# A two-layer encoder kernel: the first feed-forward matmul as seven block products, and a new order of the second

## The chip, the cores and the metric

The kernel runs on one core of one Trainium2 chip, as one program. The metric is device time in microseconds. A core has TensorE (PE, the matmul engine; PEld is its weight load), VectorE (DVE), ScalarE (ACT), GpSimd (POOL) and SyncE (SP), which here only issues transfers. Each works through its own queue in order.

## The reference, cut to what matters

Two sequences of 512 tokens and 1024 features go through two layers. Each layer ends with a squared-ReLU feed-forward part:

```
for l in range(DEPTH):                                  # DEPTH = 2
    h = x @ w_in[l]                                     # 1024 -> 5376
    ...                                                 # window attention, HGRN2, gates
    x = layer_norm(ALPHA * x + mixed @ w_out[l], ln1_g[l], ln1_b[l])
    ff = jnp.square(jax.nn.relu(x @ w_ff1[l])) @ w_ff2[l]   # 1024 -> 4096 -> 1024
    x = layer_norm(ALPHA * x + ff, ln2_g[l], ln2_b[l])
```

All of it is float32. HGRN2 is a gated linear recurrence over the tokens in both directions, done in blocks of 1 to 64 tokens.

## The kernel before, in words

**Numbers.** A float32 value is kept as a rounded part (hi, type fp32r) and a remainder (lo). One product of two such values is three matmuls: hi·hi, hi·lo, lo·hi (`mm3`, L149 to L154). `split` (L130 to L132) makes the two parts: ACT copies to hi, and POOL or DVE subtracts to get lo. `load_w` (L137) loads a weight column block of 1024 x 128 into a raw tile and splits it into a w tile. There are three raw and three w tiles.

**Tokens.** The 1024 tokens are eight rows of 128; rows 0 to 3 are group g = 0, rows 4 to 7 group g = 1. `Fm` (L156 to L188) holds an activation with features on the partitions. `put` transposes one row: twice four PE transposes into an "sm" PSUM bank, an ACT copy to hi (L185), a DVE subtraction to lo (L186). PSUM has four "mm" and four "sm" banks. `project` (L190) multiplies a weight block with one group, 24 matmuls of 128 x 128 by 128 x 512.

**A layer.** HGRN (`hgrn`, L230) projects its columns (`prep`), woven with the block recurrences (`units`) of the columns before them; `pairs` (L249) sums products within a head by a matmul with a matrix of ones, as hi and lo, first for `ox` and then for `other`, through one pair of tiles. Attention follows, then the gated output projections, `out_proj` (L868) row by row, and a layer norm for each row. Rows of x1 are transposed as they come (L899, L901).

**First feed-forward matmul (FF1).** `ff1` (L908) loads one of 32 column blocks of w_ff1, projects both groups, takes relu on ACT (L915) and the square on DVE (L916). Two blocks are a pair p, 0 to 15. `combine` (L918) makes of a pair's four 128 x 512 results (two blocks, two groups) the seven left operands of a seven-product scheme, some split already, in two pages of 1 MB, and `spill` (L929) writes them to DRAM (`hsp`).

**Second feed-forward matmul (FF2).** It is a 2 x 2 x 2 block matmul done in seven products. `PHASES` (L47) lists them: the PSUM banks ("m" or "s"; "+" adds to the phase before), the slot in `hsp`, one or two blocks of w_ff2, how these are combined, and into which quarters of the output each is folded and with what sign. A phase has 16 steps; each reads an operand from `hsp`, makes the weight operand on POOL, and splits both (`operands`, L946), two steps ahead of `products` (L969, 12 matmuls). Four 1 MB block tiles of each w_ff2 quarter are loaded by `load_block` (L936); the first two quarters from the last four pairs of FF1 on, in slots of the tiles X ("a_tile", eight of 8 KB a partition). The first phase is H_M1, whose weight operand is a sum of two blocks. `fold` (L981) adds a finished bank into the row accumulators, `close` (L994) does the layer norm and stores the row. In the last phase rows 4 to 7 are closed, and transposed as the next layer's input, while its products run; in the last four steps the products go row by row.

What sets the order: Tile's scheduler orders instructions by the program's order and by when their tiles come free; the order on each engine is then fixed. All transfers here go through SP's queue.

## Time and profile before

| | |
|---|---|
| Median of 3 runs | 3021.17 us (3017.67 to 3022.82) |
| The profiled execution's own time | 3024.58 us |
| Its span, first to last instruction | 3022.8 us |
| Mean granted TensorE clock | 0.991 |
| Matmul instructions | 16720 |
| Bytes moved by DMA | 348.75 MB |

The profile shows one execution. Busy times are sums over an engine's instructions; matmuls overlap in it, so the spacing of their starts is what one costs. "Idle before" is the time an engine sat still before an instruction, with what released it. The granted clock 1.00 is 2.4 GHz, 0.50 is 1.2 GHz.

### The profile page before, as it was taken

The page shows a single profiled execution, that of the slowest core. Times are in us where ns is not written, and L with a number is a line of the kernel's source. Part 1 is how long each engine was busy: PE and PEld are TensorE (multiplying, and loading weights), DVE is VectorE, ACT ScalarE, POOL GpSimd, SP SyncE. Part 2 cuts the span into 40 slices and gives each one's busy share as a digit, 9 for nine tenths or more (in the row PEclk, how much of TensorE's full clock was granted, in tenths as well). Part 3 has the DMA queues.
Part 4 walks back from the last instruction along what each step waited for, and adds up shares of the span by engine and source line. Part 5 has one row for each costly group of instructions (what it writes and reads, how often), then busy time and mean ns, then how long its engine had stood idle before and what let it go on. Part 6 is the DMA issues. An engine that isn't in the chain of part 4 may idle for free.

```text
span 3022.8 us, 42662 instructions
## 1 busy us (share of the span) xinstructions
PE 2949.1 (98%) x16720; PEld 2396.3 (79%) x16720; DVE 1614.0 (53%) x2813; ACT 1160.6 (38%) x1954; POOL 862.0 (29%) x532
## 2 busy tenths in 40 slices
PE   8999999999999998999999999999999999989997
PEld 6777787878888887888777777878888888878885
DVE  5777648126543444445668886570265343444447
ACT  3555647423122222343335555573232222224332
POOL 3222120112222222454542221101131222224544
PEclk9999999999999999999999999999999999999999
DMA  3111222246124356533521112322460334474334
GB/s 128 36 43 36 68 86 71 82 160 215 43 91 160 133 188 250 169 97 111 170 70 36 43 43 71 88 67 100 162 225 5 129 130 160 170 283 136 97 122 139
DMA packets 278377, 348.75 MB, mean 115 GB/s; under 512 B 16033, under 2 KB 184609, under 8 KB 269985
## 3 DMA queue, kind: packets, MB, share of 16 engines
q1 hardware_dynamic: 276880, 342.82, 34.3%
q8 instruction: 131, 2.15, 0.3%
q10 hardware_dynamic: 1296, 3.21, 0.3%
q14 instruction: 70, 0.57, 0.1%
HBM read 238.77 MB, written 100.66 MB: 112 GB/s over the span
## 4 chain that ended last, share of the span: by engine, by line
PE 83%; DVE 11%; DMA 2%; issue 1%; ACT 1%; POOL 1%; SPq 0%; POOLq 0%; ACTq 0%; DVEq 0%
PE mm L152 17%; PE mm L154 17%; PE mm L153 17%; PE mm L975 3%; PE mm L976 3%; PE sm L976 3%; PE sm L977 3%; PE sm L975 3%; PE mm L977 3%; PE mm L878 1%; PE mm L877 1%; PE mm L876 1%; PE sm L706 1%; PE sm L652 1%; PE sm L696 1%
## 5 line engine op out<-in xcount | busy, mean ns | idle before, releaser
L152 PE MATMUL mm<-X,w 128*128 128x512 f32 x2624 | 1034.4, 394 | 3.0 <-ACT w L131 2.6
L153 PE MATMUL mm<-X,w 128*128 128x512 f32 x2624 | 1027.5, 392 | 2.2 <-DVE X L186 2.0
L154 PE MATMUL mm<-X,w 128*128 128x512 f32 x2624 | 1027.8, 392 | 1.0 <-POOL w L132 1.0
L132 POOL TENSOR_TENSOR w<-raw,w 128x1024 fp32r<-128x1024 f32 (+1 forms) x179 | 419.1, 2342 | 1346.8 <-ACT w L131 1231.8
L152 PEld LDWEIGHTS mm<-X,w 128*128 128x128 f32 x2624 | 494.0, 188 | 109.2 <-ACT w L131 3.0
L154 PEld LDWEIGHTS mm<-X,w 128*128 128x128 f32 x2624 | 494.0, 188 | 102.5 <-POOL w L132 1.9
L153 PEld LDWEIGHTS mm<-X,w 128*128 128x128 f32 x2624 | 494.1, 188 | 101.9 <-DVE X L186 2.3
L131 ACT CAST w<-raw 128x1024 fp32r<-128x1024 f32 (+1 forms) x330 | 321.4, 975 | 373.8 <-PE sm L977 106.7
L916 DVE TENSOR_TENSOR X<-t 128x512 f32<-128x512 f32 x128 | 88.4, 691 | 390.4 <-ACT t L915 390.4
L132 DVE TENSOR_TENSOR w<-raw,w 128x1024 fp32r<-128x1024 f32 (+1 forms) x153 | 182.3, 1195 | 176.7 <-ACT w L131 176.6
L915 ACT ACTIVATE t<-mm 128x512 f32<-128x512 f32 x128 | 76.3, 596 | 423.0 <-PE mm L154 423.0
L965 POOL TENSOR_TENSOR raw<-X 128x512 f32<-128x512 f32 x128 | 173.6, 1358 | 227.3 <-DVE w L132 226.8
L975 PE MATMUL mm<-w 128*128 128x512 f32 x480 | 190.4, 398 | 27.0 <-ACT w L131 18.0
L976 PE MATMUL mm<-w 128*128 128x512 f32 x480 | 189.9, 396 | 0.1
L977 PE MATMUL mm<-w 128*128 128x512 f32 x480 | 189.4, 395 | 0.0
L975 PE MATMUL sm<-w 128*128 128x512 f32 x384 | 149.5, 389 | 0.0
L976 PE MATMUL sm<-w 128*128 128x512 f32 x384 | 149.4, 389 | 0.0
L977 PE MATMUL sm<-w 128*128 128x512 f32 x384 | 149.4, 389 | 0.0
L975 PEld LDWEIGHTS mm<-w 128*128 128x128 f32 x480 | 91.6, 191 | 50.2 <-ACT w L131 18.9
L359 ACT COPY bd<-Q 64x512 f32<-64x512 f32 x192 | 120.8, 629 | 14.7 <-DVE Q L429 11.8
L805 DVE TENSOR_TENSOR X<-raw,X 128x512 fp32r<-128x512 f32 x32 | 20.8, 689 | 196.0 <-ACT X L804 195.8
L963 POOL TENSOR_TENSOR w<-X,w 128x512 fp32r<-128x512 f32 x64 | 84.6, 1322 | 99.6 <-ACT w L959 98.0
(196 smaller groups left out, 3898.5 us busy)
## 6 DMA issues: line engine op xcount, KB each, us to landing
hsp<-X SPq DMA_DIRECT2D x64, 1024.0 KB
raw<-hsp SPq DMA_DIRECT2D x192, 256.0 KB
raw<-in_w_in_dram SPq DMA_DIRECT2D x84, 512.0 KB
raw<-in_w_ff_dram SPq DMA_DIRECT2D x64, 512.0 KB
X<-in_w_ff_dram SPq DMA_DIRECT2D x32, 1024.0 KB
gates<-gt SPq DMA_DIRECT2D x64, 256.0 KB
t<-gates SPq DMA_DIRECT2D x64, 256.0 KB
w<-hsp SPq DMA_DIRECT2D x24, 512.0 KB
```

The lines of the kernel that those rows point to most:

```text
L131: (first or nc.scalar.copy)(hi, src)
L132: (eng or nc.gpsimd).tensor_tensor(lo, src, hi.bitcast(F32), op=ALU.subtract)
L152: nc.tensor.matmul(ps, ah, bh, start=(i == 0), stop=False)
L153: nc.tensor.matmul(ps, ah, bl, start=False, stop=False)
L154: nc.tensor.matmul(ps, al, bh, start=False, stop=(i == n - 1))
L359: nc.scalar.copy(dst, src[hs])
L916: nc.vector.tensor_tensor(out[g], t, t, op=ALU.mult)
L963: nc.gpsimd.tensor_tensor(w[:, 1, 512:], src, w[:, 0, 512:].bitcast(F32), op=ALU.subtract)
L965: nc.gpsimd.tensor_tensor(raw[:, 512:], block(b0, k), block(b1, k), op=op)
L975: nc.tensor.matmul(ps[r], hh, wh, start=first, stop=False, **kw)
L976: nc.tensor.matmul(ps[r], hh, wl, start=False, stop=False, **kw)
L977: nc.tensor.matmul(ps[r], hl, wh, start=False, stop=stop, **kw)
```

## The change

- FF1 becomes a 2 x 2 x 2 block product too: features in two halves, the two column blocks of a pair, and the two token groups. Seven products of four 128-feature steps (12 matmuls each) replace eight. The right operands, seven of 512 x 512, are transposed and split once a layer: "11" and "21" (the two halves of group 0), "22" (a half of group 1), and four sums t1 to t4 (`sums`, `put_op`). The left operands are sums of weight blocks, made on POOL in the raw tile c and split.
- For the pairs 0 to 4 (`AHEAD`), the two products that need only group 0 ("11", "21") are done before the others, while group 1 is still being summed and transposed; their results go to DRAM (`first_sp`) and are read back in the pair.
- The row sums for the transposes lie in w tiles (rows 0, 3) and in pages (rows 1, 2). The pages of the pairs alternate between two sets, one of X tiles, one of the accumulators of rows 0 to 3, whose contents go to DRAM (`x1_sp`) and come back in FF2's first phase.
- Squares are done on ACT (relu, then square) or as one DVE operation.
- FF2 begins with H_M2 and H_M5, which use one block each; the banks of the phases are exchanged, so that the last phase is in "sm" banks. The first two blocks and the first two steps' operands are issued inside the last pair (`hook`); other blocks come during the first two phases.
- In HGRN, `pairs` is cut in two: the second ones-matmul runs one weave step later. Its tiles are six instead of four, and the gate tiles come from the same pool.

The diff, cut to its core:

```
 PHASES = (
-    ("m", H_M1, (0, 0), (1, 1), ALU.add, ((0, 0, 1), (1, 1, 1))),
     ("s", H_M2, (0, 0), None, None, ((1, 0, 1), (1, 1, -1))),
     ("m", H_M5, (1, 1), None, None, ((0, 0, -1), (0, 1, 1))),
-    ("s", H_M3, (0, 1), (1, 1), ALU.subtract, ((0, 1, 1),)),
-    ("s+", H_M6, (0, 0), (0, 1), ALU.add, ((1, 1, 1),)),
-    ("m", H_M4, (1, 0), (0, 0), ALU.subtract, ((1, 0, 1),)),
-    ("m+", H_M7, (1, 0), (1, 1), ALU.add, ((0, 0, 1),)),
+    ("s", H_M1, (0, 0), (1, 1), ALU.add, ((0, 0, 1), (1, 1, 1))),
+    ("m", H_M3, (0, 1), (1, 1), ALU.subtract, ((0, 1, 1),)),
+    ("m+", H_M6, (0, 0), (0, 1), ALU.add, ((1, 1, 1),)),
+    ("s", H_M4, (1, 0), (0, 0), ALU.subtract, ((1, 0, 1),)),
+    ("s+", H_M7, (1, 0), (1, 1), ALU.add, ((0, 0, 1),)),
 )
...
-                hi, lo = t2k(F32R), t2k(F32R)
-                for w in (ox, other):
-                    ...
+                first = ones_mm(ox)
+                next(first)
+                ps = next(first)
+                other = t2k()
+                ...
+                second = ones_mm(other)
+                next(second)
+                def crosswise():
+                    ps = next(second)
+                    ...
...
+            def put_op(name, r, nat):
+                ps = sm_ps()
+                for k in range(4):
+                    nc.tensor.transpose(ps[:, k * P:(k + 1) * P], nat[:, k * P:(k + 1) * P], ident)
+                pv = ps.rearrange("p (k t) -> p k t", t=P)
+                hi, lo = (t[:, :, r * P:(r + 1) * P] for t in ops[name])
+                nc.scalar.copy(hi, pv)
+                nc.vector.tensor_tensor(lo, pv, hi.bitcast(F32), op=ALU.subtract)
+            def sums(r, t):
+                t1, t2, t3, t4 = t
+                y0, y1 = acc[r], acc[4 + r]
+                nc.gpsimd.tensor_tensor(t3, y1[:, 512:], y1[:, :512], op=ALU.subtract)
+                nc.vector.tensor_tensor(t1, y1[:, :512], y0[:, :512], op=ALU.subtract)
+                nc.vector.tensor_tensor(t2, y1[:, 512:], t1, op=ALU.subtract)
+                nc.vector.tensor_tensor(t4, y0[:, 512:], t2, op=ALU.subtract)
+                return t
+            def left(src, eng, n=2):
+                w = w_tile()
+                split(w[:, 0, :n * 512], w[:, 1, :n * 512], src, eng)
+                ...
+            def times(ps, w, name, start=True, stop=True):
+                hi, lo = ops[name]
+                for k in range(4):
+                    ...                                   # three matmuls
...
+            for p in range(AHEAD):
+                if p >= 2:
+                    pre.append(left(w_cols(2 * p), nc.gpsimd))
+                banks[p] = mm_ps()
+                times(banks[p], pre[p][0], "11")
+                t = t512()
+                nc.scalar.copy(t, banks[p])
+                nc.sync.dma_start(first_sp[p][:, 0], t)
+                if p:
+                    finish_first(p - 1)
+                if p == 2:
+                    made.append(sums(3, in_w()))
+                if p < 4:
+                    put_second(p, made[p])
...
+            def ff1(p, hook):
+                s, h = ([part(t, i) for i in range(4)] for t in sets[p % 2])
+                a, b, c = w_cols(2 * p), w_cols(2 * p + 1), raw_tile()
+                q = slice(0, 512), slice(512, 1024)
+                if p < AHEAD:
+                    u2 = t512()
+                    nc.sync.dma_start(u2, first_sp[p][:, 0])
+                    nc.sync.dma_start(h[0], first_sp[p][:, 1])
+                else:
+                    l11, l12 = left(a, nc.gpsimd)
+                nc.gpsimd.tensor_tensor(c[:, q[0]], b[:, q[0]], b[:, q[1]], op=add)
+                nc.gpsimd.tensor_tensor(c[:, q[1]], c[:, q[0]], a[:, q[0]], op=sub)
+                s1, s2 = left(c, nc.vector)
+                nc.gpsimd.tensor_tensor(b[:, q[0]], a[:, q[0]], b[:, q[0]], op=sub)
+                nc.gpsimd.tensor_tensor(c[:, q[1]], a[:, q[1]], c[:, q[1]], op=sub)
+                s3, l22 = left(b, nc.gpsimd if p < AHEAD else nc.vector)
+                if p >= AHEAD:
+                    p1 = mm_ps()
+                    times(p1, l11, "11")
+                    u2 = t512()
+                    nc.scalar.copy(u2, p1)
+                p6 = sm_ps()
+                times(p6, s2, "t2")
+                hook(0)
+                tt(u2, u2, p6, op=add)
+                if p >= AHEAD:
+                    times(p1, l12, "21", start=False)
+                    banks[p] = p1
+                    first_done(p, h[0])
+                s4, = left(c[:, q[1]], nc.vector, 1)
+                p5 = mm_ps()
+                times(p5, s1, "t1")
+                hook(1)
+                p7 = sm_ps()
+                times(p7, s3, "t3")
+                hook(2)
+                u3 = t512()
+                tt(u3, u2, p7, op=add)
+                tt(h[3], u3, p5, op=add)
+                square_act(h[3])
+                p4 = sm_ps()
+                times(p4, l22, "t4")
+                hook(3)
+                tt(h[2], u3, p4, op=add)
+                square_act(h[2])
+                tt(s[H_M1], h[0], h[3], op=add)
+                times(p5, s4, "22", start=False)
+                tt(s[H_M5], h[0], h[2], op=add)
+                tt(h[2], h[2], h[3], op=sub)
+                tt(h[1], u2, p5, op=add)
+                square(h[1])
+                tt(s[H_M2], h[1], h[3], op=add)
+                tt(s[H_M6], h[1], h[0], op=sub)
+                nc.scalar.copy(h[1].bitcast(F32R), h[2])
+                tt(h[2].bitcast(F32R), h[2], h[1], op=sub)
...
+            early = [((i, i), c) for i in range(2) for c in range(4)]
+            def hook(i):
+                if i in (0, 2):
+                    next_block()
+                if i >= 2:
+                    feed(i - 2)
             for p in range(PAIRS):
-                ...
+                ff1(p, hook if p == PAIRS - 1 else lambda i: None)
+                spill(p)
...
-                if ph == 0 and k >= 4 and late:
+                if ph == 0 and k in (1, 4, 7, 9, 11, 13):
+                    next_block()
+                if ph == 0 and k in (8, 10, 12, 14):
+                    r = k // 2 - 4
+                    acc[r] = acc_tile(r)
+                    nc.sync.dma_start(acc[r], x1_sp[r * P:(r + 1) * P, :])
+                if ph == 1 and k % 2:
                     b, c = late.pop(0)
                     load_block(*b, c, c_tile)
```

## Rows read from the trace of the kernel before

**Rows 1.** The core's span and mean granted clock, and busy time, share of the span and instructions of four engines.
```profile
core 0: 3022.8 us, clock 0.991
...
PE 2949.1 (98%) x16720; PEld 2396.3 (79%) x16720; DVE 1614.0 (53%) x2813; ACT 1160.6 (38%) x1954; POOL 862.0 (29%) x532
```

**Rows 2.** Windows by stage: from and to (us), length, busy us (and instructions) of PE, PEld, DVE, ACT and POOL, granted clock, DMA's share, GB/s. The first five are of layer 0: two stretches of FF1, the start of FF2, its body, and its end with the turn to layer 1. The last two are FF1 and the start of FF2 in layer 1.
```profile
850.00:1000.00 150.00, 150.00 (x664) 124.24 (x663) 60.57 (x68) 32.24 (x48) 36.82 (x14) 1.00 0.40 143
1000.00:1184.00 184.00, 184.00 (x814) 152.40 (x813) 74.75 (x86) 40.29 (x59) 47.45 (x20) 1.00 0.48 170
1184.00:1240.00 56.00, 46.28 (x192) 37.34 (x191) 25.02 (x22) 17.81 (x20) 19.22 (x13) 0.91 0.88 317
1240.00:1462.00 222.00, 222.00 (x980) 183.64 (x980) 105.59 (x122) 87.27 (x113) 110.23 (x85) 1.00 0.36 107
1462.00:1528.00 66.00, 62.69 (x298) 51.39 (x297) 50.74 (x89) 23.64 (x44) 34.07 (x21) 1.00 0.52 173
...
2338.00:2684.00 346.00, 346.00 (x1530) 286.67 (x1529) 139.33 (x161) 76.36 (x114) 85.29 (x34) 1.00 0.43 154
2684.00:2740.00 56.00, 47.60 (x196) 38.27 (x195) 27.11 (x26) 18.33 (x21) 19.93 (x13) 0.91 0.87 312
```

**Rows 3.** Timeline of FF1's last block in layer 0: start, duration, engine and line. The two rows are the first and the last of 25 successive matmul starts (L152, L153, L154 in turn).
```profile
1177.65 0.39 PE L152 MATMUL mm<-X,w 128*128 128x512 f32 x1
...
1183.09 0.39 PE L152 MATMUL mm<-X,w 128*128 128x512 f32 x1
```

**Rows 4.** PE's waits: line, what released it, us in total, times, longest; and the first FF2 step of layer 0 in PE's timeline with its idle time before.
```profile
PE mm L975 <- ACT w L131: 18.0, 2, 9.7
PE sm L262 <- DVE t2k L259: 11.9, 11, 2.7
...
1207.90 1.22 PE L975 MATMUL mm<-w 128*128 128x512 f32 x2 [9.69 <-ACT w L131]
```

**Rows 5.** Transposes: eight of them as one piece of the chain of work that ended last (start, length); the duration of one (min, median, max, ns); and the window with most transposes of layer 0, columns as in rows 2.
```profile
796.26 0.87 PE sm L180 x8
...
L180 PE MATMUL sm<-ident,acc x192: 270/272/330, 796.1 to 2338.2; 128*128 128x128 f32 x192
...
820.00:838.00 18.00, 17.88 (x97) 15.00 (x96) 12.41 (x25) 6.81 (x13) 2.17 (x2) 1.00 0.00 1
```

**Rows 6.** Prices of elementwise work: groups of the page (busy us and mean ns after the bar), and single lines (min, median, max ns).
```profile
L132 POOL TENSOR_TENSOR w<-raw,w 128x1024 fp32r<-128x1024 f32 (+1 forms) x179 | 419.1, 2342 | 1346.8 <-ACT w L131 1231.8
L131 ACT CAST w<-raw 128x1024 fp32r<-128x1024 f32 (+1 forms) x330 | 321.4, 975 | 373.8 <-PE sm L977 106.7
L132 DVE TENSOR_TENSOR w<-raw,w 128x1024 fp32r<-128x1024 f32 (+1 forms) x153 | 182.3, 1195 | 176.7 <-ACT w L131 176.6
L965 POOL TENSOR_TENSOR raw<-X 128x512 f32<-128x512 f32 x128 | 173.6, 1358 | 227.3 <-DVE w L132 226.8
...
L922 DVE TENSOR_TENSOR X<-X x32: 691/692/694, 854.2 to 2679.3; 128x512 f32<-128x512 f32 x32
L985 DVE TENSOR_TENSOR acc<-acc,sm x16: 679/682/689, 1369.5 to 2913.9; 128x512 f32<-128x512 f32 x16
L185 ACT CAST X<-sm x64: 565/587/619, 6.7 to 2338.5; 128x512 fp32r<-128x512 f32 x64
```

**Rows 7.** POOL and DVE side by side in FF1's timeline (layer 0), and the durations of that DVE line over the run.
```profile
1012.24 2.69 POOL L132 TENSOR_TENSOR w<-raw,w 128x1024 fp32r<-128x1024 f32 x1 [8.19 <-ACT w L131]
1012.60 2.88 DVE L921 TENSOR_TENSOR X<-X 128x512 f32<-128x512 f32 x1
...
L921 DVE TENSOR_TENSOR X<-X x32: 682/2881/2887, 860.2 to 2685.4; 128x512 f32<-128x512 f32 x32
```

**Rows 8.** HGRN, timeline of one `pairs` in layer 0: DVE's cross products, its subtraction, and the matmul that waits for it.
```profile
142.12 1.92 DVE L253 TENSOR_TENSOR t2k<-Q,K 128x256 f32<-128x256 f32 x2
...
143.96 0.68 DVE L259 TENSOR_TENSOR t2k<-ox,t2k 128x512 fp32r<-128x512 f32 x1
...
144.69 0.50 PE L262 MATMUL sm<-t2k,ones 128*128 128x512 f32 x1 [1.00 <-DVE t2k L259]
```

**Rows 9.** The turn from layer 0 to layer 1, PE's timeline: two of the rows transposed inside the last phase, the first projection of layer 1, and DVE's part of a transposed row.
```profile
1472.06 1.03 PE L180 MATMUL sm<-ident,acc 128*128 128x128 f32 x8
...
1482.34 1.04 PE L180 MATMUL sm<-ident,acc 128*128 128x128 f32 x8
...
1509.97 0.39 PE L152 MATMUL mm<-X,w 128*128 128x512 f32 x1
...
1508.12 1.29 DVE L186 TENSOR_TENSOR X<-sm,X 128x512 fp32r<-128x512 f32 x2 [4.63 <-ACT X L185]
```

**Rows 10.** SP's queue: what its transfers waited for (us in total, times, longest); L143 is the weight load, L930 and L931 the two pages.
```profile
SPq L143 <- POOL w L132: 1268.6, 150, 85.1
...
SPq L930 <- DVE X L921: 94.3, 10, 10.6
SPq L931 <- DVE X L927: 55.3, 32, 4.2
```

More of the change, by code (lines that the diff above doesn't have):

```diff
@@ L555, in hgrn @@
                 nu = blank()
-                weave(units(p, u, prev), prep(p + 1, nu) if p < 3 else gate(5))
+                weave(units(p, u, prev), prep(p + 1, nu) if p < 3 else gate(t2k, 5))
                 prev, u = u, nu
@@ L789, in tile_encoder_trunk @@
         last = l == DEPTH - 1
[L790 to L795 removed]
+        gate = gate_maker(l, xT)
+        hgrn(l, xT, gate)
+        if not last:
+            lower_bounds()
+        attention(l, xT, gate)
         w_hg = [load_w([w_proj_hgrn[l][:, m * P:(m + 1) * P]]) for m in range(2)]
@@ L897, in tile_encoder_trunk @@
                 acc.append(y)
+                if j == 4:
+                    open_op("11", c_tile)
+                    open_op("21", c_tile)
                 if j >= 4:
-                    x1.put(j - 4, acc[j - 4])
-            for j in range(8 - 4, 8):
-                x1.put(j, acc[j])
+                    put_first(j - 4)
+                if j in (4, 5):
+                    pre.append(left(w_cols(2 * (j - 4)), nc.gpsimd))
+                if j == 6:
+                    made.append(sums(0, in_w()))
             hid = hsp[l]
@@ L929, in spill @@
-            def spill(p, h, s):
-                nc.sync.dma_start(hid[p][:, H_M1:H_M6 + 1], s)
-                nc.sync.dma_start(hid[p][:, H_M3:], h)
+            for name, tile in (("22", c_tile), ("t2", a_tile), ("t1", a_tile), ("t3", a_tile), ("t4", a_tile)):
+                open_op(name, tile)
+            sets = [[page(c_tile), page(c_tile)]]
+            for r in (1, 2):
+                t = sets[0][r - 1]
+                made.append(sums(r, [t[:, i] for i in range(4)]))
+            banks = {}
@@ new lines, in tile_encoder_trunk, with part, store @@
+            finish_first(AHEAD - 1)
+            for r in range(4):
+                nc.sync.dma_start(x1_sp[r * P:(r + 1) * P, :], acc[r])
+            sets.append([
+                [acc_tile(0).rearrange("p (k t) -> p k t", t=512) for _ in range(2)] for _ in range(2)
+            ])
+            def part(t, i):
+                return t[i // 2][:, i % 2] if isinstance(t, list) else t[:, i]
+            def store(dst, t):
+                if isinstance(t, list):
+                    for i in range(2):
+                        nc.sync.dma_start(dst[:, 2 * i:2 * i + 2], t[i])
+                else:
+                    nc.sync.dma_start(dst, t)
```

148 lines of the change are left out of this document (81 added, 67 removed).

## The prediction

> **What bounds the kernel now.** I read the page's busy times first: TensorE (PE) is busy 98% of the span, DVE 53%, ACT 38%, POOL 29%, and the granted clock averages 0.991 [rows 1]. So the time is PE's, if that share is real at each stage. The windows by stage say that it is: in the first feed-forward matmul (FF1) PE is busy 150.00 of 150, 184.00 of 184 and 346.00 of 346 us, all at clock 1.00, and so it is through most of the second one (FF2); between them are windows with PE idle and a clock of 0.91 [rows 2]. Inside FF1 the timeline shows what a matmul costs: from one L152 matmul at 1177.65 to another 24 matmuls later at 1183.09 is 5.44 us, 0.2267 us each [rows 3]; the 390 ns of the group rows overlap. 1536 of them make 348.2 us a layer. Last, PE's waits: the longest is ACT's cast at the start of FF2, 18.0 us in two times, one of them the 9.69 us gap at 1207.90; then 11.9 us for the ones-matmul L262 in the HGRN stage [rows 4].
>
> **What the change costs, part by part** (both layers together unless said).
>
> *Fewer products.* Each of 16 pairs of FF1 columns did 96 matmuls and now does 7 x 12 = 84. That is 192 fewer a layer, 384 in all: 384 x 0.2267 = **-87.1 us**. They are on the path, since nothing else runs out there.
>
> *More transposes.* Seven operands of 512 x 512 take 112 transposes a layer against 64. Eight back to back advance the chain by 0.87 us, 0.109 each, though each lasts 272 ns, and the stretch with most of them keeps clock 1.00 [rows 5]. 96 x 0.109 = **+10.5**. In their copies out of PSUM, ACT's 0.587 and DVE's 0.69 lie beside PE work. The Trainium skill, page "TensorE: Matmul & The Clock Gate", Part 4, gives about 275 ns for a transpose in a kernel and says that transposes don't engage the full clock; charged so, the term would be 26.4 and the sum 16 us worse. The trace agrees with the duration and not with the clock.
>
> *The stretch before the pairs* (five products pairs in advance, four rows of sums). PE has 120 matmuls and 80 transposes, 27.2 + 8.7 = 35.9 us a layer. DVE has 20 subtractions out of PSUM and 12 sums at 0.69, 22 us; ACT 20 x 0.587 and some 12 for casts and copies, 24; POOL 4 x 1.36 + 3 x 2.34 = 12.5 [rows 6]. All are covered on average. But a row's five groups of transposes are 2.2 us of PE and 3.45 of DVE, and four banks hold them: 0 to 1.25 us a burst, eight bursts, 0 to +10. I take **+4**, nearer to no stall since matmuls lie between the bursts. Row 7's layer norm, once followed by its transposes, is now needed three pairs later.
>
> *The pairs themselves.* Pairs 5 to 15: PE 84 x 0.2267 = 19.0 us. POOL has four additions and a split, 4 x 1.36 + 2.34 = 7.8; DVE two splits at 1.2 and thirteen operations at 0.69, 11.4; ACT about 9. Pairs 0 to 4 have only 60 matmuls, 13.6 us, for POOL's 7.8 and DVE's 1.2 + 13 x 0.69 = 10.2. Here engines could collide. In the timeline POOL's subtraction L132 starts at 1012.24 and lasts 2.69, and DVE's addition L921, begun at 1012.60, lasts 2.88; the same operation beside an idle POOL (L922) takes 0.69 every time, and an addition that reads PSUM (L985) 0.68 at most 0.69, POOL busy or not [rows 6, 7]. So DVE operations with both sources in SBUF stand still while POOL works. Of DVE's 10.2 us, five PSUM readers are free and 6.7 are exposed: 6.7 + 7.8 = 14.5 us that cannot overlap, 0.9 over PE's 13.6. With no overlap at all it is 18.0, 4.4 over. Ten such pairs: +9 to +44. I take **+15**, near the lower end, because DVE's exposed work comes at the end of a pair and POOL's at its start. The lower bound for the range is 0, if work done ahead covers pair after pair. The Trainium skill, page "SBUF — State Buffer", section "SBUF: two separate sides", says the same as a rule: the shared pair of ports is an exclusive lock held for the whole instruction, and a DVE operation with two SBUF inputs takes it. The rule speaks against this change, which puts POOL and DVE on the same tiles; rival B is its full price. Pairs 5 to 15 need 7.8 + 7.9 = 15.7 of 19.0: **0**, with PE as the cover; no gain is possible there and +1 a pair, 22, is the far bound.
>
> *Waits inside a pair.* The last product adds into the bank that DVE must first read. After the fifth product ends, two PSUM additions (1.4 us) stand before it, and the sixth product gives 2.7. Weight tiles: four a pair go through three slots; the tile of the last product takes the slot that the third product frees, 8.2 us before its use. Raw tiles are three, all used by one pair, so the next loads start only when POOL and DVE are done with them; the second weight column is free about 4.7 us into a pair and needed, added, cast and split (4.9 us) at 21.8, so the load may take 12 us. SP's queue also holds two pages of 1 MB a pair, 2.1 MB at the 317 GB/s of the busiest window, 6.6 us [rows 2]: the load fits behind them. Cost **0**; if that cover is gone, rival D.
>
> *FF1 to FF2.* Before, the first FF2 step needed two blocks, loaded behind the last pages, and its reads came behind those on SP: in the windows PE lost 9.7 + 8.4 us idle, and 192 + 196 matmuls took 46.28 + 47.60 busy instead of 43.5 + 44.4, at clock 0.91: 24 us [rows 2, 4]. Now the first step wants one block, its load is issued after the second product of the last pair, 13.6 us before FF2, and the first two operand tiles are made in that pair. The reads of steps 5 and 6 still fall behind the last pages (6.6 us). Bounds -24 and 0; I take **-21**, since 13.6 us covers a block's 3.3 us with room.
>
> *HGRN.* L262's wait: DVE did two cross products (L253, 1.92 us) before the subtraction L259 that the matmul needed [rows 8]. They now come after, and the second pair of matmuls waits for the next step of the weave. PE's 11.9 us is the most it can give, 0 the least; I take **-9**, as the unwoven first block keeps part of its wait. The gate tiles share six buffers with it; a sigmoid there is off the path.
>
> *The turn of the layer.* The last FF2 phase moves from the "mm" banks to the "sm" banks, which the transposes of the next layer's input use. Before, rows 4 to 6 were transposed inside that phase (1472.06, 1482.34) and the next layer's L152 followed the last product at 1509.97 [rows 9]. Now its four banks are all taken until the first fold, so three rows come in the last 8 us: six half rows of 0.5 + 0.59 + 0.68 us, 11 if nothing hides them, 0 if the other rows' products do. I take **+4**, once. Other folds keep their number and price. The reload of four rows (2 MB) is issued 20 us ahead of its use: 0.
>
> **Sum.** -87.1 + 10.5 + 4 + 15 - 21 - 9 + 4 = -83.6, against the profiled execution's 3024.58 (span 3022.8): 2941. The median of the runs, 3021.17, lies 3.4 lower: **2937 us**.
>
> **Rivals.**
> A, the forecast: FF1 stays PE's. Its own range is 2914 to 2955: all stalls at 0 below, +18 above.
> B, POOL and DVE become the bound: no overlap in the first five pairs, 44 instead of 15, and 7.8 + 11.4 = 19.2 against 19.0 in the others, +4: 2970. For it: L921's 2.88, median of 32. Against: PSUM readers pass, and DVE's work is spread by the products.
> C, the gap before FF2 stays, as pages, blocks and reads share SP's queue: +21, 2958. For it: 317 GB/s there. Against: the 13.6 us of lead.
> D, on the other side, loads: with three raw tiles, if a weight load issued in a pair lands 16 us later, behind pages that themselves wait on SP, s2 comes at 9.6 + 16 = 25.6 instead of 21.8, 3.8 us late; 32 pairs are 122 us, 3059. It turns slower from 2.8 us a pair. For it: SP already waits 1268.6 us in all for raw tiles, and pages wait for DVE in the same queue [rows 10]. Against: half the load time of that window is enough.
> E, the transposes don't overlap and cost their own 272 ns each, 26 us instead of 10.5: +16, 2953. Against: [rows 5]. (It is also where the Trainium skill's figure above would lead.) That the products are not seven is excluded by the code.
>
> **Chances.** A 0.62, B 0.18, C 0.12, D 0.04, E 0.04. The predicted time is A's. The range 2905 to 2978 holds A, B, C, E and reaches below A by the HGRN wait's rest and a full 24 us at FF2. About 0.2% (6 us) is what a measurement of this kernel can tell from no change. All cases but D are below 3015: faster 0.95, within 0.02 (a milder D), slower 0.03.
>
> **What would show it.** Right: 112 transposes and 1344 FF1 matmuls a layer; FF1 windows with PE busy all the time at clock 1.00 except in the first five pairs, which last 14.5 to 16 us each; no PE wait over 2 us at the first FF2 step; L262's rows without waits. Wrong: DVE operations of 2 us or more throughout pairs 5 to 15 with PE waiting for splits (B), an idle window of 10 us before FF2 (C), PE waiting for casts that waited for raw tiles (D).

## The result, and the profile after

The changed kernel takes 2969.60 us (median of 4 runs, 2968.18 to 2971.12) against 3021.86 of the kernel before: ratio 0.9832, 95% interval 0.9817 to 0.9847. It is 52 us faster, where 84 were forecast; the time lies in the stated range, 32.6 us above the predicted one.

The span and the busy times, as in [rows 1]:

```profile
core 0: 2966.1 us, clock 0.993
...
PE 2874.6 (97%) x16432; PEld 2335.9 (79%) x16432; DVE 1746.0 (59%) x3011; ACT 1285.1 (43%) x2138; POOL 978.6 (33%) x646
```

PE has 288 instructions fewer: 384 matmuls less, 96 transposes more. It is still the busiest, but its idle time rose from 73.7 to 91.5 us (span less busy) though the span is shorter. The windows of layer 0, columns as in [rows 2], say where:

```profile
840.00:882.00 42.00, 39.56 (x201) 31.92 (x199) 15.39 (x22) 20.08 (x34) 18.03 (x12) 1.00 0.41 132
882.00:926.00 44.00, 40.27 (x169) 32.62 (x169) 32.19 (x42) 15.71 (x23) 21.49 (x14) 0.96 0.61 206
926.00:960.00 34.00, 32.31 (x143) 26.45 (x142) 22.96 (x29) 14.95 (x21) 16.55 (x12) 1.00 0.67 242
960.00:1000.00 40.00, 40.00 (x178) 33.14 (x177) 23.15 (x32) 16.88 (x24) 17.67 (x12) 1.00 0.45 160
...
1140.00:1180.00 40.00, 36.75 (x151) 28.78 (x150) 21.64 (x26) 15.56 (x27) 11.54 (x8) 0.96 0.85 307
...
1200.00:1430.00 230.00, 230.00 (x1016) 190.30 (x1015) 119.89 (x129) 89.20 (x103) 115.02 (x88) 1.00 0.46 146
1430.00:1500.00 70.00, 60.16 (x270) 48.87 (x269) 50.60 (x84) 23.08 (x41) 32.54 (x21) 0.93 0.49 160
```

From 960 on, FF1 is PE's alone, as in the kernel before; so is the body of FF2. Four stretches are not: the one before the pairs (to 882), the short pairs (to 940), the start of FF2 (1140 to 1180) and the turn of the layer (1430 to 1500). PE's waits name them, as in [rows 4]:

```profile
PE sm L1143 <- DMA w<-hsp: 8.4, 7, 2.7
PE mm L933 <- DVE X L1083: 7.5, 4, 2.5
...
PE sm L183 <- DVE rs L206: 5.3, 1, 5.3
...
PE mm L933 <- DVE acc L1083: 5.2, 3, 1.8
...
PE mm L934 <- DVE X L892: 4.6, 2, 2.3
PE sm L1145 <- DVE w L1128: 4.4, 2, 2.2
PE sm L261 <- DVE t2k L257: 3.1, 4, 1.5
```

L933 to L935 are FF1's matmuls, L1143 to L1145 FF2's. L1083 (a page's sum, read from a bank) and L892 (a transpose's subtraction) are new in this list; the 18.0 us wait for the cast early in FF2 is gone, and HGRN's 11.9 us are now 3.1 (L261). The 8.4 us for reads from `hsp` stand in FF2's last phase; they were 5.6 in the kernel before.

The marks below are starts of PE rows: of the first `out_proj` matmul, of the first FF2 matmul, of the first projection of layer 1, and so on. Each column is the time from one mark to the next.

| kernel | to `out_proj`, layer 0 | to FF2 | to layer 1 | to `out_proj`, layer 1 | to FF2 | to the end |
|---|---|---|---|---|---|---|
| before | 741.7 | 442.8 | 325.5 | 730.4 | 442.8 | 339.7 |
| changed | 737.8 | 418.8 | 329.1 | 729.0 | 419.7 | 331.7 |
| no loads (e1) | 739.1 | 414.7 | 329.5 | 727.3 | 417.2 | 331.8 |
| narrow pages (e2) | 740.5 | 418.1 | 327.7 | 728.2 | 418.2 | 333.0 |
| mm banks (e3) | 739.0 | 418.7 | 319.1 | 729.1 | 420.2 | 331.5 |
| old HGRN (e4) | 741.9 | 419.6 | 326.8 | 729.5 | 419.9 | 330.7 |
| splits swapped (e5) | 738.5 | 416.3 | 328.4 | 728.5 | 416.2 | 331.1 |
| b on DVE (e6) | 738.2 | 417.0 | 327.9 | 726.4 | 416.5 | 331.3 |
| t3 on DVE (e7) | 739.8 | 415.7 | 329.2 | 726.0 | 415.2 | 333.0 |
| pages on ACT (e8) | 739.6 | 418.5 | 330.4 | 729.3 | 418.4 | 333.3 |
| three edits (e9) | 739.0 | 412.6 | 319.5 | 727.4 | 413.0 | 334.4 |
| old phases (e10) | 738.5 | 424.0 | 323.0 | 726.6 | 423.7 | 332.5 |
| three, 4 ahead (e11) | 737.9 | 412.8 | 319.5 | 726.7 | 411.7 | 331.5 |

Stages that two kernels have in common scatter by 2 to 4 us, those of FF1 (second and fifth column) by 2, so only larger differences, or those with a wait that comes or goes, are read.

### The profile page after: what moved, and what is told of

Read it like the earlier page. It is cut to its first block, busy times and chain, and to the rows that moved or that the text cites. A ratio compares the mean times of both kernels' runs of the same rounds, so it can differ in the third digit from the quotient of the medians.

```text
span 2966.1 us, 42845 instructions
## 1 busy us (share of the span) xinstructions
PE 2874.6 (97%) x16432; PEld 2335.9 (79%) x16432; DVE 1746.0 (59%) x3011; ACT 1285.1 (43%) x2138; POOL 978.6 (33%) x646
## 4 chain that ended last, share of the span: by engine, by line
PE 81%; DVE 8%; DMA 4%; issue 4%; POOL 2%; ACT 2%; SPq 1%; POOLq 0%; ACTq 0%; DVEq 0%
PE mm L155 11%; PE mm L157 11%; PE mm L156 11%; PE mm L935 3%; PE mm L934 3%; PE mm L933 3%; PE mm L1144 3%; PE mm L1143 3%; PE mm L1145 3%; PE sm L1145 3%; PE sm L1144 3%; PE sm L1143 3%; PE sm L933 2%; PE sm L934 2%; PE sm L935 2%
## 5 line engine op out<-in xcount | busy, mean ns | idle before, releaser
L155 PE MATMUL mm<-X,w 128*128 128x512 f32 x1600 | 634.9, 397 | 5.6 <-ACT w L134 5.2
L135 POOL TENSOR_TENSOR w<-raw,w 128x1024 fp32r<-128x1024 f32 (+1 forms) x157 | 347.7, 2215 | 884.4 <-ACT w L134 831.1
L156 PE MATMUL mm<-X,w 128*128 128x512 f32 x1600 | 628.5, 393 | 2.5 <-DVE X L189 2.3
L157 PE MATMUL mm<-X,w 128*128 128x512 f32 x1600 | 627.1, 392 | 1.2 <-POOL w L135 1.2
L134 ACT CAST w<-raw 128x1024 fp32r<-128x1024 f32 (+1 forms) x394 | 375.7, 954 | 401.2 <-PE mm L1145 116.6
L135 DVE TENSOR_TENSOR w<-raw,w 128x1024 fp32r<-128x1024 f32 (+1 forms) x239 | 267.2, 1118 | 247.2 <-ACT w L134 246.9
L155 PEld LDWEIGHTS mm<-X,w 128*128 128x128 f32 x1600 | 301.4, 188 | 72.9 <-ACT w L134 6.1
L157 PEld LDWEIGHTS mm<-X,w 128*128 128x128 f32 x1600 | 301.6, 189 | 63.9 <-POOL w L135 2.3
L156 PEld LDWEIGHTS mm<-X,w 128*128 128x128 f32 x1600 | 301.7, 189 | 62.5 <-DVE X L189 2.6
L1133 POOL TENSOR_TENSOR raw<-X 128x512 f32<-128x512 f32 x128 | 166.1, 1298 | 172.5 <-DVE w L135 172.5
L933 PE MATMUL mm<-X,w 128*128 128x512 f32 x512 | 202.2, 395 | 12.7 <-DVE X L1083 7.5
L934 PE MATMUL mm<-X,w 128*128 128x512 f32 x512 | 200.7, 393 | 4.6 <-DVE X L892 4.6
L935 PE MATMUL mm<-X,w 128*128 128x512 f32 x512 | 200.9, 392 | 2.5 <-POOL w L135 2.5
L1143 PE MATMUL sm<-w 128*128 128x512 f32 x480 | 189.1, 394 | 11.0 <-DMA w<-hsp 8.4
L1145 PE MATMUL sm<-w 128*128 128x512 f32 x480 | 187.9, 393 | 4.5 <-DVE w L1128 4.4
L1144 PE MATMUL sm<-w 128*128 128x512 f32 x480 | 188.5, 393 | 1.9 <-POOL w L1131 1.5
L933 PE MATMUL sm<-X,w 128*128 128x512 f32 x384 | 149.6, 390 | 0.0
L934 PE MATMUL sm<-X,w 128*128 128x512 f32 x384 | 149.5, 389 | 0.0
L1143 PE MATMUL mm<-w 128*128 128x512 f32 x384 | 149.5, 389 | 0.0
L1145 PE MATMUL mm<-w 128*128 128x512 f32 x384 | 149.4, 389 | 0.0
L1144 PE MATMUL mm<-w 128*128 128x512 f32 x384 | 149.4, 389 | 0.0
L935 PE MATMUL sm<-X,w 128*128 128x512 f32 x384 | 149.4, 389 | 0.0
```

The source lines that it names most:

```text
L134: (first or nc.scalar.copy)(hi, src)
L135: (eng or nc.gpsimd).tensor_tensor(lo, src, hi.bitcast(F32), op=ALU.subtract)
L155: nc.tensor.matmul(ps, ah, bh, start=(i == 0), stop=False)
L156: nc.tensor.matmul(ps, ah, bl, start=False, stop=False)
L157: nc.tensor.matmul(ps, al, bh, start=False, stop=(i == n - 1))
L933: nc.tensor.matmul(ps, w[:, 0, k], hi[:, k], start=(start and k == 0), stop=False, **kw)
```

## The experiments

The changed kernel was not timed again beside these runs, and the ratios' intervals are 0.15% wide on each side. A difference of 5 us is therefore read from the traces.

**What sets the short pairs.** Pairs 0 to 4 should take PE 13.6 us. From one L1083 to the next they take 15.4, 15.5 and 15.6, then 12.8. This is the third L1083 and the wait behind it, in the timeline of the changed kernel:

```profile
908.20 1.29 POOL L1055 TENSOR_TENSOR raw<-raw 128x512 f32<-128x512 f32 x1 [4.06 <-DMA raw<-in_w_ff_dram]
...
909.57 1.62 POOL L1056 TENSOR_TENSOR raw<-raw 128x512 f32<-128x512 f32 x1
...
911.22 1.05 ACT L134 CAST w<-raw 128x1024 fp32r<-128x1024 f32 x1 [2.28 <-POOL raw L1056]
912.31 1.23 DVE L135 TENSOR_TENSOR w<-raw,w 128x1024 fp32r<-128x1024 f32 x1 [2.27 <-ACT w L134]
...
913.45 0.68 DVE L1082 TENSOR_TENSOR t<-t,sm 128x512 f32<-128x512 f32 x1
...
914.17 0.69 DVE L1083 TENSOR_TENSOR X<-t,mm 128x512 f32<-128x512 f32 x1
...
915.00 0.47 PE L933 MATMUL mm<-X,w 128*128 128x512 f32 x1 [1.59 <-DVE X L1083]
```

The last product (915.00) adds into a bank that L1083 must read first. L1082's own product had long ended: PE had since run the whole next one (2.7 us), up to about 913.2. L1082 could have started at about 910.5 and started at 913.45, because DVE's queue has the split of c (912.31) ahead of L1082, and that split belongs to the next pair: it waited for the cast, the cast for POOL's two sums, the first of these for a load.

The first interval, 15.4, has another reason. PE waited 2.47 us for the first L1083, up to 884.14, and then the granted clock fell to 0.50 from 885.5 to 888.9. Seven matmuls there start 0.43 us after the one before instead of 0.23, which costs 1.4 us; behind the second L1083 PE hardly waits (columns as in [rows 2]):

```profile
885.50:888.90 3.40, 3.40 (x10) 2.62 (x9) 1.96 (x2) 2.32 (x4) 2.37 (x1) 0.50 0.53 144
```

For the other intervals there are three theories: the loads' 4 us (T1), POOL and DVE excluding each other (T2), the order in DVE's queue (T3, formed after the first two runs).

*e1, no loads in pairs 1 to 4.*

```
-  a, b, c = w_cols(2 * p), w_cols(2 * p + 1), raw_tile()
+  if not 0 < p < AHEAD:
+      kept[:] = w_cols(2 * p), w_cols(2 * p + 1)
+  (a, b), c = kept, raw_tile()
```

Expected:


> The changed kernel, but the pairs 1 to 4 of FF1 load no weights: they go on with the two raw tiles of pair 0 (their results are then not those of the reference; every other instruction is kept). Theory T1 (loads): the three raw tiles set the length of the short pairs: a pair's second weight tile is free only after POOL's split, its load takes 4 us, POOL's additions, ACT's cast and DVE's split follow, and DVE's bank reads L1082 and L1083 stand behind that split in DVE's queue. Without loads the starts of pairs 1 to 4 stand 13.6 to 14.2 us apart instead of 15.5, and the time falls by 10 to 16 us from 2969.6, to about 2956. Theory T2 (POOL and DVE exclude each other, 14.5 us of exposed work a pair): the pairs stay at 15.0 to 15.6 us and the time at 2967 to 2971.

Measured: 2960.04 us, 0.9799 [0.9784, 0.9814]. The time fell by nearly as much as T1 wanted, but not where it wanted: the pairs are still 15.4, 15.3 and 15.3 apart. FF1 is 4.1 and 2.5 us shorter; in layer 0 the first wait of 2.47 us and the stretch at half clock behind it do not occur. The rest is in the stages' scatter. T1 falls as the cause of the pairs' length in the changed kernel. The timeline of e1 shows what takes the load's place:

```profile
905.06 1.67 POOL L1059 TENSOR_TENSOR raw<-raw 128x512 f32<-128x512 f32 x1 [3.03 <-DVE w L135]
...
916.04 1.81 DVE L1096 TENSOR_TENSOR X<-X 128x512 f32<-128x512 f32 x1 [1.45 <-ACT X L1039]
```

POOL's first sum (L1059 here) now waits for DVE's split of s4, which frees c and stands behind the end of the pair before; and L1096 (L1092 of the changed kernel) takes 1.81 us, not 0.68, beside POOL's split of b (914.89 to 917.30).

*e2, narrow page operations in pairs 2 to 4* (as an example, L1090; five of them so).

```
-  tt(s[H_M1], h[0], h[3], op=add)
+  tt(s[H_M1][:, :nx], h[0][:, :nx], h[3][:, :nx], op=add)   # nx = 64 for 2 <= p < AHEAD
```

Expected:


> The changed kernel, but in the pairs 2 to 4 the five DVE operations of the pages with both sources in SBUF (L1090, L1092, L1093, L1096, L1097) work on 64 of 512 columns (the rest of these page slots keeps old values). That takes 5 x 0.55 = 2.8 us of DVE's exposed work from each of six pairs. T2 (lock): 14.5 - 2.8 = 11.7 us is below PE's 13.6, so the pairs 2 to 4 fall from 15.5 to about 13.7 us and the time by some 10 us, to 2959. T1 (loads): the chain through the raw tile keeps its length, the pairs stay at 15.2 to 15.6 us and the time at 2966 to 2971.

Measured: 2969.24 us, 0.9828 [0.9814, 0.9843]. L1083 comes ahead of the page operations of its pair, so the narrow ones lie in the interval after pair 2's L1083 and in the next: 15.2 us in layer 0 and 15.4 in layer 1, against 15.6 in the changed kernel, and 12.7 against 12.8. As T1 said, and a miss for T2 as put: a shorter sum of exposed work hardly shortens the pair. But it does not clear POOL either, since a narrow operation that starts beside POOL's split is held up as a wide one is: it takes 1.33 us instead of 0.23 and ends at 922.29, when the split (from 919.81 to 922.21) has ended:

```profile
920.96 1.33 DVE L1093 TENSOR_TENSOR X<-X 128x64 f32<-128x64 f32 x1 [1.91 <-ACT X L1039]
922.33 0.23 DVE L1094 TENSOR_TENSOR X<-X 128x64 f32<-128x64 f32 x1
```

*e5, the splits of b and c exchanged between POOL and DVE in the short pairs.*

```
-  s1, s2 = left(c, nc.vector)
+  s1, s2 = left(c, nc.gpsimd if p < AHEAD else nc.vector)
-  s3, l22 = left(b, nc.gpsimd if p < AHEAD else nc.vector)
+  s3, l22 = left(b, nc.vector)
```

Expected:


> The changed kernel, but in the pairs 0 to 4 the split of c goes to POOL and that of b to DVE. T3 (order in a queue): in those pairs DVE's queue holds the next pair's split of c right before L1082 and L1083, which the last product of this pair waits for; that split waits for ACT's cast, POOL's two additions and the freeing of c. With the split of c on POOL, DVE's queue goes from L1099 to L1082 directly. Then the short pairs fall from 15.5 to 13.6 to 14.2 us, the PE waits for L1083 (12.7 us in all) go, and the time falls by 10 to 14 us from 2969.6, to about 2957. T2 (lock): POOL's and DVE's exposed work is the same sum, 14.5 us: the pairs stay at 15.2 to 15.6 us, the time at 2967 to 2971.

Measured: 2962.56 us, 0.9821 [0.9805, 0.9837]; by time alone this is not told apart from the changed kernel. In the trace the waits for L1083 are gone in these pairs, which stand 13.6, 14.1, 17.5 and 13.6 us apart: two pairs at PE's length, as T3 said, and then a new wait, for POOL, which now has the split of c (2.4 us) in the chain to the first product:

```profile
914.68 0.50 PE L933 MATMUL sm<-X,w 128*128 128x512 f32 x1 [0.40 <-ACT w L134]
917.15 0.80 PE L935 MATMUL sm<-X,w 128*128 128x512 f32 x1 [1.74 <-POOL w L135]
```

Behind these the granted clock is 0.50 from 916.7 to 920.1, so the 17.5 is 13.6, 2.1 of waits and some 1.7 of clock (an estimate, half of that stretch). FF1 gained 2.5 and 3.5 us, not 5 to 7.

*e6, both splits on DVE in the short pairs.*

```
-  s3, l22 = left(b, nc.gpsimd if p < AHEAD else nc.vector)
+  s3, l22 = left(b, nc.vector)
```

Expected:


> The changed kernel, but in the pairs 0 to 4 the split of b goes to DVE and that of c stays there. T2 (lock): the exposed sum falls from 14.5 to 5.4 + 7.9 = 13.3 us, below PE's 13.6, and POOL's longest operation, behind which L1092 stood for 1.8 us, is gone: pairs of 13.7 to 14.3 us, 2957 to 2960. T3 (order in a queue): the split of c stays ahead of L1082; b is free some 1 us earlier, and with it the load: pairs of 14.8 to 15.5 us, 2964 to 2970.

Measured: 2959.19 us, 0.9805 [0.9791, 0.9820]; pairs of 14.4, 14.3 and 14.4. The split of c still stands ahead of L1082, and PE still waits there, but 0.5 us instead of 1.6:

```profile
900.67 0.47 PE L933 MATMUL mm<-X,w 128*128 128x512 f32 x1 [0.50 <-DVE acc L1083]
```

So both have a part: T2's numbers nearly came here and T3's did not; in e5 it was rather the other way round. DVE's order hands the next pair's lateness to this pair's last product (e5), and POOL's longest operation, with what stands behind it, makes that lateness (e6). Which share of the 1.1 us is the shared access and which is POOL's own time in the chain is not separated here. For the first interval the clock counts too: e6 has the same wait before it (2.53 us, to 886.28), and the clock stays at 1.00. Of the 0.8 us that are left over PE's 13.6, the load's share is open: in e6 POOL's first sum waits for its load (7.70 us, to 893.87), and no run takes the loads out of e6.

**The stretch before the pairs.** PE's wait for L892 at 832.50; timeline of POOL and DVE in the changed kernel:

```profile
824.88 3.42 POOL L901 TENSOR_TENSOR X<-acc 128x512 f32<-128x512 f32 x2 [2.46 <-PE mm L947]
...
827.08 2.37 DVE L903 TENSOR_TENSOR X<-acc,X 128x512 f32<-128x512 f32 x2
...
831.77 0.67 DVE L892 TENSOR_TENSOR X<-sm,X 128x512 fp32r<-128x512 f32 x1
...
832.50 0.51 PE L934 MATMUL mm<-X,w 128*128 128x512 f32 x1 [2.31 <-DVE X L892]
```

Sums of x1's rows stand ahead of the subtraction that the first product needs. L901 is t3; POOL ends it at 828.30, and of the two L903 the one that began before that took 1.77 us, the other 0.68.

*e7, the sum t3 on DVE.*

```
-  nc.gpsimd.tensor_tensor(t3, y1[:, 512:], y1[:, :512], op=ALU.subtract)
+  nc.vector.tensor_tensor(t3, y1[:, 512:], y1[:, :512], op=ALU.subtract)
```

Expected:


> The changed kernel, but the fourth sum of each row of x1 (t3) is made on DVE instead of POOL. In the stretch before the pairs PE waits 2.3 us for L892 at 832.5 while DVE's sums L902 and L903 take 1.78 and 2.37 for two. If POOL's sum held these up (lock), they fall to 0.69 each and the wait of L892 to under 1 us: 3 us less over two layers, and up to 3 more from the waits at 844.9 and 857.7; 2964 to 2967. If the order of DVE's queue alone does it, the two more sums on DVE make it 0.7 us worse a layer: 2970 to 2972.

Measured: 2959.34 us, 0.9808 [0.9793, 0.9822], better than either theory said; FF1 gained 3.1 and 4.5 us. In this run the first `out_proj` matmul comes 2.0 us later (739.8 against 737.8); counted from it, DVE does more operations and is done 2.1 us earlier:

```profile
828.05 0.68 DVE L901 TENSOR_TENSOR X<-acc 128x512 f32<-128x512 f32 x1
828.65 0.68 DVE L903 TENSOR_TENSOR X<-acc,X 128x512 f32<-128x512 f32 x1
...
832.38 0.50 PE L934 MATMUL mm<-X,w 128*128 128x512 f32 x1 [0.20 <-DVE X L892]
```

Every sum takes 0.68 or 0.69, and the wait of 2.31 is 0.20. In layer 1 the changed kernel's granted clock was 0.50 for 3.4 us at this wait (from 2308.9); here it is not, which is part of the 4.5. Here the exclusion of POOL and DVE is the cause: moving a POOL operation onto the busier engine shortened the stretch. The Trainium skill, page "SBUF — State Buffer", section "SBUF: two separate sides", calls it an exclusive lock held for the whole instruction; L903's 2.37 us for two operations beside POOL and 0.68 each without agree.

**The turn of the layer.** In the changed kernel:

```profile
1466.94 0.66 PE L183 MATMUL sm<-ident,acc 128*128 128x128 f32 x4
1474.49 1.09 PE L183 MATMUL sm<-ident,acc 128*128 128x128 f32 x4 [5.26 <-DVE rs L206]
...
1472.09 1.04 ACT L134 CAST w<-raw 128x1024 fp32r<-128x1024 f32 x1 [4.79 <-DMA raw<-in_w_in_dram]
1473.04 0.58 ACT L188 CAST X<-sm 128x512 fp32r<-128x512 f32 x1
...
1473.65 0.69 DVE L189 TENSOR_TENSOR X<-sm,X 128x512 fp32r<-128x512 f32 x1 [5.33 <-ACT X L188]
```

No row is transposed before the first fold at 1466; PE then stands still for 5.3 us. DVE is not what is short there: it stands still for 5.33 us itself. The copy of the transposed half row (L188), which the subtraction L189 waits for, stands in ACT's queue behind a cast of the next layer's weights, and that cast waits 4.79 us for its load.

*e3, these transposes into the mm banks.*

```
-  nxt_x.put(3 + k // 3, acc[3 + k // 3])
+  nxt_x.put(3 + k // 3, acc[3 + k // 3], mm_ps)     # put: ps = (bank or sm_ps)()
```

Expected:


> The changed kernel, but the rows 4 to 7 of the next layer's input are transposed into the mm banks, which are free in the last FF2 phase. Theory: the turn lost 10 us because these transposes had to wait for the first fold of the sm banks and then shared DVE with the layer norms. Then three rows go back inside the phase, the gap of 5.3 us before a transpose at 1474 goes, and the time falls by 6 to 9 us from 2969.6, to about 2962. Rival: the turn is set by DVE's layer norms or by the late reads of the last phase's operands, which cost 4.9 us there: then the time stays within 2 us.

Measured: 2960.03 us, 0.9806 [0.9790, 0.9823]. The stretch from FF2 to layer 1 fell by 10.0 us, to 319.1; the rows are back inside the phase, and the wait is gone:

```profile
1449.44 1.03 PE L183 MATMUL mm<-ident,acc 128*128 128x128 f32 x8
...
1461.41 1.04 PE L183 MATMUL mm<-ident,acc 128*128 128x128 f32 x8
```

The whole stretch from FF2 to layer 1, the changed kernel first, e3 second (columns as in [rows 2]):

```profile
1156.50:1485.70 329.20, 316.11 (x1378) 259.12 (x1378) 178.22 (x211) 126.19 (x167) 164.70 (x120) 0.98 0.53 174
1157.70:1476.80 319.10, 310.55 (x1377) 255.15 (x1376) 171.15 (x199) 124.41 (x165) 162.16 (x119) 1.00 0.55 177
```

Of the 10 us, 4.5 are idle time of PE and 5.6 are busy time. The changed kernel has the granted clock at 0.50 for 13.7 us in three parts, from 1165.4, 1452.1 and 1472.6; the last two go with waits of PE of 2.71 and 5.26 us (to 1450.68 and 1474.49) that e3 does not have, and e3 has no such part. The first lies at FF2's start, behind a wait that e3 has too (2.21 us, to 1165.11), and is no effect of the banks: up to 1.7 us (an estimate, half its length). So the exchange of the banks cost 8 to 10 us, and without it FF2 with its start is 6.4 us shorter than before (319.1 against 325.5).

**The start of FF2.** First the kernel before. The wait of 9.69 us in [rows 4] is not at the first step: that one follows FF1 at 1184.45 without a wait. PE has done 60 matmuls, five steps, when it stops, and the cast that it waits for needs the sixth step's operand, whose read went out behind the last page and three blocks:

```profile
1197.50 1.41 SPq L955 DMA_DIRECT2D raw<-hsp  x3
...
1206.80 1.99 ACT L131 CAST w<-raw 128x1024 fp32r<-128x1024 f32 x2 [15.61 <-DMA raw<-hsp]
```

In layer 1 it is the same (8.36 us, to 2705.25, with FF2 begun at 2683.1). The changed kernel's rows:

```profile
1140.10 0.39 SPq L1106 DMA_DIRECT2D X<-in_w_ff_dram  x1
...
1142.59 1.70 SPq L1030 DMA_DIRECT2D hsp<-X  x2
1144.38 2.63 SPq L1106 DMA_DIRECT2D X<-in_w_ff_dram  x2
...
1155.87 1.14 ACT L1127 CAST w<-X 128x512 fp32r<-128x512 f32 x2 [1.92 <-DMA X<-in_w_ff_dram]
...
1157.89 0.50 PE L1144 MATMUL sm<-w 128*128 128x512 f32 x1 [0.85 <-POOL w L1131]
1164.27 0.96 PE L1145 MATMUL sm<-w 128*128 128x512 f32 x3 [2.24 <-DVE w L1128]
```

The block that the first step's cast waits for is the one issued at 1144.38, behind another block (1140.10) and two pages (1142.59) and together with a third block; it lands 11.5 us later, just too late. The second wait is for the split of the next operand, behind the last pair's work on DVE.

*e8, the last four pages through ACT's queue* (which otherwise carries a part of the kernel's first loads and last stores).

```
-  store(hid[p][:, H_M1:H_M6 + 1], s)
+  store(hid[p][:, H_M1:H_M6 + 1], s, nc.scalar if p >= PAIRS - 2 else nc.sync)
```

Expected:


> The changed kernel, but the pages of the last two pairs are stored through ACT's queue instead of SP's. Theory: at the start of FF2 PE waits because the first block (issued at 1144.4, landed at 1155.9) stands behind 2 MB of pages in SP's queue. With a queue of its own it lands 3 to 6 us earlier, POOL's L1131 no longer comes late, and the FF2 start loses 1 to 2 us instead of 6 in each layer: 2960 to 2965. Rival: both queues feed the same 16 engines and the block shares their rate with the pages; it lands less than 2 us earlier and the time stays at 2968 to 2971.

Measured: 2968.35 us, 0.9838 [0.9824, 0.9853], no gain. The rival holds: the pages go out on ACT's queue at 1144.32 and 1145.69, the block at 1144.52, and it lands at 1155.96, as before.

```profile
1155.96 0.62 ACT L1127 CAST w<-X 128x512 fp32r<-128x512 f32 x1 [5.14 <-DMA X<-in_w_ff_dram]
```

From the block's issue to its landing the DMA engines are busy all the time, in the changed kernel (first) and in e8 (second; DMA's share and GB/s are the last columns):

```profile
1144.00:1156.00 12.00, 12.00 (x55) 9.94 (x53) 4.59 (x7) 3.66 (x7) 0.00 (x0) 1.00 1.02 390
1144.00:1156.00 12.00, 12.00 (x55) 9.93 (x54) 4.51 (x8) 2.93 (x6) 0.00 (x0) 1.00 1.01 386
```

In which of the two queues the bytes stand did not matter; that they are under way together fits both runs. That the block would land in time if it went out ahead of the pages, as the one at 1140.10 did, was not tried.

*e10, the old order of the phases in the changed kernel.*

```
-  early = [((i, i), c) for i in range(2) for c in range(4)]
+  early = [(b, c) for c in range(4) for b in ((0, 0), (1, 1))]
   ...                                              # PHASES as in the kernel before
-  if ph == 0 and k in (1, 4, 7, 9, 11, 13):
+  if ph == 0 and k in (0, 1, 3, 5, 7, 9):
```

Expected:


> The changed kernel with the old order of the FF2 phases (two-block product H_M1 first, last phase in the mm banks), the first blocks loaded in turns of the two quarters and the later ones at steps 0, 1, 3, 5, 7, 9. It undoes the second half of the change alone. The turn gets its old banks back, 10 us better, as in the run with the transposes moved. The first step needs two blocks instead of one, 1 MB or 3.3 us more behind the same pages, and POOL's sum before the cast (1.3 us): 3 to 6 us worse at each FF2 start. So 2966 to 2972; against the run with the transposes in the mm banks (2960) it shows what the single-block start is worth, 6 to 12 us. Rival: the start of FF2 is set by the tail of the last pair on DVE (L1128 waits 2.2 us there), not by blocks: then this run equals that one, 2960.

Measured: 2973.10 us, 0.9844 [0.9827, 0.9860]. FF2 comes 5.2 and 4.0 us later than in the changed kernel, and its first steps wait 3.58 and 1.89 us, where the changed kernel waits 0.85 and 2.24:

```profile
1162.49 2.08 PE L1143 MATMUL mm<-w 128*128 128x512 f32 x4 [3.58 <-ACT w L134]
```

Part of it is the clock: 0.50 for 10.2 us from 1162.4 and for 6.8 from 2637.0, against 3.4 us from 1165.4 and none there in layer 1. Against e3, which has the same banks free at the turn, e10 is 13 us slower by the medians; from the first `out_proj` matmul on it loses 9.2 us in layer 0 and 4.5 in layer 1. This is what the single-block start, with its order of loads, is worth here, some 6.5 us a layer on average; the banks took 8 to 10 of it back.

**HGRN.** *e4, the old `pairs`* (the old function, its call, and six buffers kept).

```
-  tail = pairs(r, vt)
-  yield
-  tail()
-  continue
+  pairs(r, vt)
```

Expected:


> The changed kernel with the HGRN part undone (the old pairs, no step between its two halves; the six buffers kept). By the marks of the two traces the HGRN stages gained 3.9 + 1.4 = 5.3 us: 2975 is expected if the new order of pairs gave that. If it gave the 9 us of the forecast and something else cost 4, about 2979. If the six buffers gave it, 2970.

Measured: 2972.61 us, 0.9841 [0.9826, 0.9855]: 3 us, not resolved by time. In the trace PE waits 12.3 us for the ones-matmul, against 3.1, and `out_proj` of layer 0 comes at 741.9, where the kernels with the new order have 737.8 to 740.5; in layer 1 its stage takes 729.5, against 726.0 to 729.3.

```profile
PE sm L265 <- DVE t2k L262: 12.3, 12, 2.7
```

The wait is cured, 9 us of it. What comes of it in time is a few us, within the stages' scatter.

**Edits together.** *e9* has the edits of e3, e6 and e7; *e11* has them and `AHEAD = 4`. Expected:


> The changed kernel with three of the earlier edits together: transposes of the last FF2 phase in the mm banks, the split of b on DVE in the short pairs, t3 on DVE. The three losses lie in different stretches (turn, short pairs, stretch before them); if each is a loss of its own, the gains add: 9.7 + 7.6 + 7.4 = 24.7 us against the changed kernel beside the same runs, about 2945. If they share a cause (DVE is what is short, and t3 and the split of b load it further), the sum is smaller: 2950 to 2957.

> The run e9 with four pairs in advance instead of five: one short pair a layer becomes a long one, the matmuls are the same in number. Short pairs still cost 0.8 us over PE's 13.6 there, and the stretch before them has one unit less to put between the transposes. If the short pairs' price decides, 1 to 3 us faster than e9; if the cover of the transposes does, equal or slower by up to 3.

Measured: e9 2948.60 us, 0.9762 [0.9747, 0.9776]; e11 2945.71 us, 0.9748 [0.9733, 0.9763]. Both are faster than the kernel before and the changed one. The three gains add in the main (21 of 24.7 us). e11 is the version to keep, but its gain over e9, 3 us, lies inside the intervals and is not in FF1, whose stages take 412.8 and 411.7 us against 412.6 and 413.0: what four pairs in advance instead of five are worth is not shown.

## Why the prediction was right and wrong

The bound was read rightly: FF1 was PE's, 384 matmuls at 0.2267 us left it, and from pair 5 on PE is busy all the time, pairs of 19.0 us as worked out. The time lies in the range because the range is wide (73 us, it reaches to rival B); five of the six terms came out worse than put, and the sum is a third short. The marks give each term its measured size, to 2 to 4 us:

| term | forecast | measured | from |
|---|---|---|---|
| FF1: matmuls and transposes | -76.6 | -76.6 | taken as forecast: pairs of 19.0 us, transposes 0.11 us apart |
| stretch before the pairs | +4 | about +13 | starts of PE rows later than back to back, 6 to 8 us a layer |
| short pairs | +15 | about +17 | the rest of FF1, whose sum is -24.0 and -23.1; the waits for L1083 are 12.7 of it |
| FF2's start | -21 | -14 | -6.4 (e3 against before) and -8.0 (layer 1) |
| HGRN | -9 | -5 | -3.9 and -1.4 |
| turn of the layer | +4 | +10 | e3; up to 1.7 of it belongs to FF2's start |
| sum | -83.6 | -56.7 | spans 3022.8 and 2966.1; the rounded terms add to -56 |

*The stretch before the pairs* was sized from averages ("all are covered on average") and from banks. What cost most was one subtraction behind sums that POOL held up: without them FF1 is 7.6 us shorter (e7). The argument on POOL and DVE stood in the text, but was applied to the pairs alone.

*The short pairs* came out near the number, for a reason that the text had excluded. "Waits inside a pair" were put at 0: two PSUM additions, 1.4 us, under a product of 2.7. The additions take 1.4 us; what failed is that they start when their product ends. They start when the work ahead of them in DVE's queue is done, and this is the next pair's. The bound of 14.5 us from exposed work was the wrong model: with 2.8 us of it taken away, an interval of 15.6 became 15.2 to 15.4 (e2). The chain of queues (e5), with POOL's longest operation in it (e6), is nearer. No term was put for the clock, which falls to 0.50 behind the first of these waits and costs 1.4 us there.

*FF2's start*: the wait before was read as the first step's, for two blocks; it was the sixth step's, for an operand read behind page and blocks. Of the new start the text says: "its load is issued after the second product of the last pair, 13.6 us before FF2", and "13.6 us covers a block's 3.3 us with room". The block took 11.5, with pages and other blocks under way, and the lead was 12. The step that failed is the price of one transfer alone, in a stretch where the DMA engines are never free. A third of rival C came, 7 of 21 us: that pages and blocks are under way together fits, that they share one queue does not matter (e8).

*The turn*: the rows came after the first fold as forecast, and the size is near the far bound (8 to 10 of 11), but not because of half rows that nothing hides. The cost was not in the text: a copy in ACT's queue behind a cast that waits for the next layer's weights (5.3 us of PE), and half clock at PE's waits.

*HGRN*: the wait went as said; a new wait in the weave took part of it back (L505 waits 6.3 us for DVE's L272 in the changed kernel; neither the kernel before nor e4 has that wait).

Rival B gave 2970, the measured time to 0.4 us, but its mechanism did not happen: short pairs are 15.5 us, not 18.0, and long ones 19.0, not 19.2. Rival D did not show, as e1 removed the loads and left the pairs. Rival E is excluded by the starts: the transposes of the new stretch stand 0.11 us apart, not 0.27.

## What to carry to other kernels

An operation of the critical chain starts when its engine's queue reaches it, not when its input is there: for each such operation, name what stands ahead of it in its queue and what that waits for, above all the next iteration's work. When a change takes PSUM banks for one use, list who else took banks of that tag there; moving four transposed rows to the other banks gave 8 to 10 us. After a wait of PE read the granted clock too: the matmuls behind the wait can lose more: 1.4 us in the first short pair. Where POOL and DVE work on SBUF side by side in a stretch that is short of slack, the slower engine's operation can cost more than doing it on the busier one.

## What the runs showed of the hardware

A load of 1 MB that was issued behind 2 MB of stores and another load landed after 11.5 us, and equally late when the stores went through another engine's queue (1155.87 and 1155.96), with the DMA engines busy all that time (390 and 386 GB/s). A DVE sum that began beside a POOL sum took 1.77 us, and 0.68 when POOL's sum was itself moved to DVE. At PE's waits of 2.47, 2.71 and 5.26 us in the changed kernel the granted clock went to 0.50 for 3.4 to 6.8 us, and matmuls started 0.43 us apart instead of 0.23; at one of 2.53 us in e6 it stayed at 1.00. Between 827.5 and 864 the changed kernel has 88 transposes, 0.11 us apart, among matmuls, at a granted clock of 1.00.
